# Layer 1's three modulation products: two of them out of the RWKV recurrence, one to the routing, one to the latent's mLSTM, one ahead of layer 1

## The chip, the core and the metric

The kernel runs on one core of one Trainium2 chip. The metric is the device time of one launch in microseconds (us); lower is better. One core has a matrix engine (PE in the profile; its weight loads are PEld), three engines for elementwise work (DVE, ACT, POOL), and SP, which here issues the loads of weights. Each engine runs its instructions in the order in which the program put them.

## The reference

One token sequence of 256 tokens and width 1024 goes through two blocks. Block 1 is RWKV-7 time mixing with its recurrence `wkv7_scan`, a dense SwiGLU, block attention (MoBA) and a mixture of 8 experts. Block 2 has two layers on the latent `x` and a context `xc` of 256 tokens. Every norm of block 2 is modulated by a vector that comes from a product with a large matrix:

```python
silu_c = jax.nn.silu(c)
silu_cc = jax.nn.silu(c_ctx)
for l in range(DEPTH):
    mod_x = (silu_c @ ada_w[l] + ada_b[l])[:, None, :]
    mod_c = silu_cc @ ada_w[l] + ada_b[l]
    sh1, sc1, g1, sh2, sc2, g2 = jnp.split(mod_x, 6, axis=-1)
    hx = modulate(rms_norm(x, norm_g[l, 0]), sh1, sc1)
    ...
```

`ada_w[l]` is 1024 x 6144, 25 MB in f32, and it meets two vectors only. Layer 0 of block 2 is neighbourhood attention beside a bidirectional mLSTM (`even_mixer`), layer 1 is multi-head latent attention (`odd_mixer`); each has a convolutional FFN behind it.

## The kernel before, in words

All weights come from HBM in f32, 512 KB at a time, into a ring of six buffers (`wraw`); ACT and DVE split each into a high and a low part (`whi`, `wlo`), and PE multiplies with both, so a linear layer is three sums of products (high by high, high by low, low by high). SP issues a load into a ring buffer as soon as the buffer's last reader is done; it works through its loads strictly in their order.

The modulation is cut into six products `ada(l, j)` (line 1310), j a third of layer l's columns. One has eight steps: each loads 1 MB of `ada_w` into two ring buffers, which PE reads directly, in plain f32: four matmuls of 128 rows, 32 columns and 512 elements, one to each quarter of the PSUM tile's partitions (line 1320, helper L262). After the eighth, ACT copies the PSUM tile (`adar`), PE turns it with four transposes (helper L282), and DVE adds the bias into `modT`. That is the ninth step. The PSUM tile, one of the four of set 1, is held from the first step to the last.

`Filler` (line 1334) holds the six products as generators, in the order (0,0), (0,1), (0,2), (1,0), (1,1), (1,2). `st["fill"].step(n, keep)` advances the first one by up to n steps, and stops when only `keep` products are left. The places of the calls set where the steps are written: eight in `rwkv_proj`; in `block1_front` one at every `ADA_EVERY`-th yield of the recurrence `wkv` (304 yields) up to yield 286, and one at every second from there; then at the end of `moba` and in `moe_route` (the routing).

A scheduling layer then orders what each engine gets: it keeps the written order as a priority but lets an instruction go ahead where it reckons that an engine would wait. So a step's four matmuls are often parted.

From line 2056 on, the latent's chain (`x_chain`: PSUM set 0) and the context's (`ctx_rest`: set 1) are interleaved by the numbers of `SIDE`: for each yield of the latent, so many of the context's. The context's FFN of layer 0 so runs beside the latent's mLSTM (`mlstm`, line 1601, called in `even_x`, line 1764) and beside the border between the layers (`x_chain`, lines 1995 and 1996), where the latent goes through the residual, a norm (squares on ACT: tile `sq`), a scaling on DVE (`xscr`) and transposes on PE before layer 1's first product, with `od_w_dq` (its matmuls show as `hT0h,whi`; the context's up-projections as `hT1h,whi`, down-projections as `whi,hid`).

Of the kernel before, what the change touches and what calls it, by code (L numbers as in the profile page):

```python
# [574 lines left out]
    yield  # L575


ADA_EVERY = 10
WKV_END = 286
A_RATES = (1.0, 0.8, 1.0, 0.0)  # L580
WKV_AR = 3
# [466 lines left out]
def moe_route(N, st, ch=0):  # L1048

    nc, a, c = N.nc, N.a, N.c  # L1050
    h = st["h"]
    x = N.act_slots(2, 3, "h3T")
    N.to_T(ch, lambda tb: h[:, tb * D:(tb + 1) * D], x)
    st["fill"].step(1)
    yield
    w = N.wload(a["moe_router"][0], KD, NE)
    p = N.ps(ch)
    N.mmT(p[:NE, 0:T], w, x, KD, 0, NE)
    lg = N.t256("lg")
    N.act(lg[:NE], p[:NE, 0:T])  # L1060
    p2 = N.ps(ch)
    for tb in range(2):
        N.tr(p2[:, tb * NE:(tb + 1) * NE], lg[:NE, tb * P:(tb + 1) * P])
    lt = N.cstp.tile([P, 2, NE], F32, name="logits")
    N.act(lt, p2[:, 0:2 * NE].rearrange("p (b e) -> p b e", b=2))
    st["fill"].step(2)
    yield

    gt, eq = N.t256("gt8"), N.t256("eq8")
    g4 = gt[:, 0:128].rearrange("p (b e f) -> p b e f", b=2, e=NE)  # L1070
    e4 = eq[:, 0:128].rearrange("p (b e f) -> p b e f", b=2, e=NE)
    le, lf = bc(lt, 3, NE), bc(lt, 2, NE)
    N.tt(g4, lf, le, ALU.is_gt)
    N.tt(e4, lf, le, ALU.is_equal)
    N.tt(e4, e4, bc(c["lt8"].rearrange("p (e f) -> p e f", e=NE), 1, 2), ALU.mult)
    N.tt(g4, g4, e4, ALU.add)
    rank = N.sm(16, "rank").rearrange("p (b e) -> p b e", b=2)
    nc.vector.tensor_reduce(rank, g4, axis=AX.X, op=ALU.add)
    s1 = N.sm(16, "sel1").rearrange("p (b e) -> p b e", b=2)
    s2 = N.sm(16, "sel2").rearrange("p (b e) -> p b e", b=2)  # L1080
    N.ts(s1, rank, 0.0, op0=ALU.is_equal)
    N.ts(s2, rank, 1.0, op0=ALU.is_equal)
    v = N.sm(4, "topv")
    tmp = N.sm(16, "topt").rearrange("p (b e) -> p b e", b=2)
    for i, s in ((0, s1), (1, s2)):
        N.tt(tmp, s, lt, ALU.mult)
        nc.vector.tensor_reduce(v[:, 2 * i:2 * i + 2], tmp, axis=AX.X, op=ALU.add)
    yield
    d = N.sm(2, "topd")
    N.tt(d, v[:, 2:4], v[:, 0:2], ALU.subtract)  # L1090
    N.act(d, d, AF.Exp)
    w1 = N.sm(2, "w1")
    N.ts(w1, d, 1.0, op0=ALU.add)
    nc.vector.reciprocal(w1, w1)
    w2 = N.sm(2, "w2")
    N.tt(w2, d, w1, ALU.mult)
    gates = N.cstp.tile([P, 2, NE], F32, name="gates")
    sel = N.cstp.tile([P, 2, NE], F32, name="sel")
    pos = N.cstp.tile([P, 2, NE], F32, name="pos")
    N.tt(gates, s1, bc(w1, 2, NE), ALU.mult)  # L1100
    N.tt(tmp, s2, bc(w2, 2, NE), ALU.mult)
    N.tt(gates, gates, tmp, ALU.add)
    N.tt(sel, s1, s2, ALU.add)
    p = N.ps(ch)
    st["fill"].step(100)
    N.mm(p[:, 0:NE], c["tri_strict"], sel[:, 0, :], True, True)
    N.mm(p[:, NE:2 * NE], c["ones"], sel[:, 0, :], True, False)
    N.mm(p[:, NE:2 * NE], c["tri_strict"], sel[:, 1, :], False, True)
    N.mm(p[:, 2 * NE:3 * NE], c["ones"], sel[:, 0, :], True, False)
    N.mm(p[:, 2 * NE:3 * NE], c["ones"], sel[:, 1, :], False, True)  # L1110
    nc.vector.tensor_copy(pos, p[:, 0:2 * NE].rearrange("p (b e) -> p b e", b=2))
    yield
    mx = N.sm(1, "maxn")
    nc.vector.tensor_reduce(mx, p[:, 2 * NE:3 * NE], axis=AX.X, op=ALU.max)
    cnt = N.cstp.tile([P, 1], I32, name="count")
    nc.vector.tensor_copy(cnt, mx)
    hh, hl = N.slot(4, "h_hi", F32R), N.slot(5, "h_lo", F32R)
    for i in range(0, 2 * D, 512):
        s = slice(i, i + 512)
        N.split(hh[:, s], hl[:, s], h[:, s])  # L1120
    st.update(hh=hh, hl=hl, gates=gates, sel=sel, pos=pos, cnt=cnt)
    acc = N.slot(6, "moe_acc")
    st["acc"] = acc
    yield
# [252 lines left out]
def modulated(N, st, ch, src, l, which, r, slots, scr):  # L1377

    q = 3 * which
    sc = N.sm(8, "scale")  # L1380
    N.ts(sc, st["mod"].piece(l, q + 1, r), 1.0, op0=ALU.add)
    N.tt(sc, sc, N.v["norm_g_2"][:, (l * 4 + 2 * which) * 8:(l * 4 + 2 * which) * 8 + 8], ALU.mult)
    sh = N.sm(8, "shift")
    N.nc.vector.tensor_copy(sh, st["mod"].piece(l, q, r))
    for tb in range(2):
        s = slice(tb * D, (tb + 1) * D)
        rs = inv_rms(N, src[:, s])
        N.ts(scr[:, s], src[:, s], rs)
    x = N.act_slots(slots[0], slots[1], f"hT{ch}")
    N.to_T(ch, lambda tb: scr[:, tb * D:(tb + 1) * D], x, scale=sc, bias=sh)  # L1390
    return x
# [368 lines left out]
def even_x(N, st, ch, x, S):  # L1760
    nc, a, c = N.nc, N.a, N.c
    yield from even_proj(N, st, ch, x, S, "Ex")
    E, Ec = st["Ex"], st["Ec"]
    yield from paced(mlstm(N, st, ch, E, st["CT"], st["ms"], True), SIDE["mlstm"])

    bias = [N.slot(S["b"][i], f"bias{i}") for i in range(2)]
    for jt in range(2):
        for rr in range(2):
            r0 = 7 - 2 * jt - rr
            nc.scalar.dma_start(bias[jt][rr * 64:rr * 64 + 64].rearrange("p (h x) -> p h x", h=8),  # L1770
                                a["rpb"][:, :, r0:r0 + 4].rearrange("q h r k -> q h (r k)"))
    o = N.act_slots(S["h"][0], S["h"][1], "yx")
    mlstm_out(N, st, ch, E, o)
    yield 8 * SIDE["bias"]
    qo, kv, kvc = E["qo"], E["kv"], Ec["kv"]

    def score(pr, hh, qt, p):
        q = slice(hh * 64, hh * 64 + 64)
        l = qo[q, pr * T + qt * P:pr * T + (qt + 1) * P]
        N.mm(p[:, 0:T], l, kv[q, pr * T:(pr + 1) * T], True, True)  # L1780
        N.mm(p[:, T:2 * T], l, kvc[q, pr * T:(pr + 1) * T], True, True)

    def vsrc(pr, hh, b):
        t = kv if b < 2 else kvc
        o_ = 1024 + (b % 2) * 512 + (2 * pr + hh) * 64
        return t[:, o_:o_ + 64]

    def biased(pr, hh, qt, p, S_):
        h = 2 * pr + hh
        N.stt(S_[:, 0:T], p[:, 0:T], 0.125, bias[qt][:, h * T:(h + 1) * T], ALU.mult, ALU.add)  # L1790
        N.act(S_[:, T:2 * T], p[:, T:2 * T], AF.Copy, scale=0.125)
    yield from paced(attend(N, ch, o, 4, 4, score, vsrc, 0.125, biased, ch2=1 - ch), SIDE["na"])
    st["yx_act"] = o
# [187 lines left out]
SIDE = dict(moba_in=0, moba=1, moba_out=0, start=5, mlstm=1.25, bias=0.5, na=0.5, res0=3, end0=5, mla=1.5)  # L1981


def x_chain(N, st, out, ch=0):

    a, nc = N.a, N.nc
    h = st["h"]
    x = modulated(N, st, ch, h, 0, 0, 0, (2, 3), N.slot(4, "xscr"))
    yield SIDE["start"]
    yield from even_x(N, st, ch, x, dict(qo=4, kv=5, ml=6, kh=12, h=(2, 3), b=(6, 10)))  # L1990
    yield from out_proj(N, st, ch, st["yx_act"], a["ev_w_out_2"][0], h, 0, 0, 4)
    y = N.slot(12, "ffy0")
    x = modulated(N, st, ch, h, 0, 1, 0, (2, 3), y)
    yield SIDE["res0"]
    yield from ffn_conv(N, st, ch, h, 0, 0, x, (4, 5, 6), (12, 10), y)
    x = modulated(N, st, ch, h, 1, 0, 0, (2, 3), N.slot(4, "xscr2"))
    yield SIDE["end0"]
    N.load_consts("consts_m", small(N, "consts_m"))
    yield from mla_x(N, st, ch, x, dict(lat=4, q=(5, 6), k=(12, 7), v=13, o=(2, 3)))
    yield from out_proj(N, st, ch, st["ox_act"], a["od_w_o_2"][0], h, 1, 0, 4)  # L2000
    y = N.slot(12, "ffy1")
    x = modulated(N, st, ch, h, 1, 1, 0, (2, 3), y)
    yield
    yield from ffn_conv(N, st, ch, h, 1, 0, x, (4, 5, 6), (12, 10), y,
                        lambda tb: nc.sync.dma_start(out[tb * P:(tb + 1) * P], h[:, tb * D:(tb + 1) * D]))
# [13 lines left out]
def paced(g, n):  # L2019
    for _ in g:  # L2020
        yield n
# [11 lines left out]
def block1_front(N, st):  # L2033

    ada_setup(N, st)
    fill = st["fill"] = Filler(ada(N, st, l, j) for l, j in ((0, 0), (0, 1), (0, 2), (1, 0), (1, 1), (1, 2)))
    for _ in rwkv_proj(N, st):
        pass
    for i, _ in enumerate(wkv(N, st)):
        if i % ADA_EVERY == 3 if i < WKV_END else i % 2:  # L2040
            fill.step(1, 1)
    side = ctx_even(N, st)
    for g, r in zip((rwkv_out, ffn_dense, moba, moe_route), A_RATES):
        rated(g(N, st), side, r)
    advance(side, 1000)
# [25 lines left out]
```

## Time and profile before

| | us |
|---|---|
| median of 3 runs | 2863.96 (2863.25 to 2868.87) |
| the profiled execution | 2869.28 |
| its span in the trace | 2867.5 |
| PE busy in the span | 2763.4 (96%) |
| DVE busy | 2243.2 (78%) |
| ACT busy | 1773.8 (62%) |

The span runs from the first to the last instruction of the trace; the profiled execution is 1.8 us longer, and that stays as it is. All rows below are of this execution. A row of the timeline gives the start, the time until the group's last instruction ends, engine, line, operation, what it writes and reads, its form and how many there are; in brackets the idle time of the engine before it and what ended it. An f32 matmul stands in the trace as two rows, so a step's four matmuls are x8. A busy PE is one with a matmul under way; successive matmuls overlap, so the distance from start to start is what one costs the next.

### The profile page before, as it was taken

The numbers are of one execution on the slowest core, as the hardware profiler recorded it, in microseconds if no ns is written. First come the engines' busy times: TensorE is split into PE (matmuls) and PEld (weight loads), VectorE is DVE, ScalarE is ACT, GpSimd is POOL, SyncE is SP. The second block draws the span as 40 slices with busy tenths as digits, with TensorE's granted clock in tenths as the row PEclk, the third lists the DMA queues.
The fourth block names the chain that finished last, engine by engine and source line by source line (L and its number), as shares of the span: only waits on it lengthen the run. The fifth ranks groups of instructions, "written<-read, shape, count | busy, mean of one in ns | idle before, by whom it ended". The sixth has DMA issues, their size and how long they took to land. (4 is left out here: it accounts for less than half of the span.)

```text
span 2867.5 us, 49977 instructions
## 1 busy us (share of the span) xinstructions
PE 2763.4 (96%) x18356; PEld 2268.0 (79%) x18356; DVE 2243.2 (78%) x4406; ACT 1773.8 (62%) x3601; POOL 67.0 (2%) x87
## 2 busy tenths in 40 slices
PE   8999999999999999999999999989989999989898
PEld 8677589897866777777777777768877899877897
DVE  7366385577577999999999999986687787886767
ACT  5223255444566887887787878766446665666654
POOL 0011100000000000000000000000000000000000
PEclk9999999999999999999999999999999999999999
DMA  7444666544539999999999999976543465521453
GB/s 244 161 142 155 214 193 183 178 139 134 158 96 336 357 333 352 348 356 335 346 361 335 346 349 361 348 250 176 162 129 114 137 198 178 158 78 45 147 185 125
DMA packets 357231, 641.16 MB, mean 224 GB/s; under 512 B 24785, under 2 KB 153937, under 8 KB 356978
## 3 DMA queue, kind: packets, MB, share of 16 engines
q1 hardware_dynamic: 348768, 625.58, 64.8%
q10 hardware_dynamic: 8210, 12.30, 1.4%
q8 instruction: 146, 2.39, 0.3%
q14 instruction: 107, 0.88, 0.1%
HBM read 636.76 MB, written 1.05 MB: 222 GB/s over the span
## 5 line engine op out<-in xcount | busy, mean ns | idle before, releaser
L250 DVE TENSOR_TENSOR wlo<-wraw,whi 128x512 fp32r<-128x512 f32 (+1 forms) x2181 | 1377.8, 685 | 259.0 <-ACT whi L247 198.3
L247 ACT ACTIVATE whi<-wraw 128x512 fp32r<-128x512 f32 (+1 forms) x2181 | 1215.0, 622 | 428.7 <-PE ps L262 320.9
L262 PE MATMUL ps<-whi,xg 128*128 128x512 f32 x1792 | 499.2, 398 | 1.9 <-ACT whi L247 1.9
L262 PEld LDWEIGHTS ps<-whi,xg 128*128 128x128 f32 x1792 | 327.2, 188 | 86.0 <-ACT whi L247 25.0
L262 PE MATMUL ps<-wlo,xg 128*128 128x512 f32 x896 | 295.1, 398 | 0.0
L262 PE MATMUL ps<-whi,hT 128*128 128x512 f32 x896 | 260.2, 401 | 0.0
L262 PE MATMUL ps<-hT0h,whi 128*128 128x256 f32 (+2 forms) x872 | 216.7, 286 | 3.8 <-ACT whi L247 3.3
L262 PE MATMUL ps<-hT0l,whi 128*128 128x256 f32 (+2 forms) x872 | 216.7, 285 | 0.1
L262 PEld LDWEIGHTS ps<-wlo,xg 128*128 128x128 f32 x896 | 168.1, 188 | 55.9 <-DVE wlo L250 20.4
L262 PE MATMUL ps<-whi,hid 128*128 128x512 f32 x704 | 190.4, 406 | 10.3 <-DVE cv L259 7.1
L262 PEld LDWEIGHTS ps<-whi,hT 128*128 128x128 f32 x896 | 164.4, 188 | 32.6
L262 PEld LDWEIGHTS ps<-hT0h,whi 128*128 128x128 f32 (+2 forms) x872 | 168.2, 193 | 4.9 <-ACT whi L247 3.5
L262 PEld LDWEIGHTS ps<-hT0l,whi 128*128 128x128 f32 (+2 forms) x872 | 168.3, 193 | 0.9 <-DVE hT0l L250 0.4
L262 PE MATMUL ps<-wlo,hT 128*128 128x512 f32 x448 | 168.5, 416 | 0.0
L262 PEld LDWEIGHTS ps<-whi,hid 128*128 128x128 f32 x704 | 131.7, 191 | 45.0 <-issue 15.6
L262 PE MATMUL ps<-hT1h,whi 128*128 128x256 f32 (+1 forms) x504 | 127.7, 290 | 12.2 <-ACT whi L247 11.6
L259 DVE SCALAR_TENSOR_TENSOR cv<-ps,vecs,cv 128x255 f32<-128x255 f32 x264 | 124.8, 479 | 12.7 <-ACT cv L247 11.5
L262 PE MATMUL ps<-hT1l,whi 128*128 128x256 f32 (+1 forms) x504 | 125.7, 286 | 0.0
L262 PE MATMUL ps<-hT0h,wlo 128*128 128x256 f32 (+2 forms) x872 | 123.9, 283 | 1.6 <-DVE wlo L250 1.5
L262 PEld LDWEIGHTS ps<-hT0h,wlo 128*128 128x128 f32 (+2 forms) x872 | 113.0, 191 | 2.8 <-DVE wlo L250 2.4
L262 PEld LDWEIGHTS ps<-hT1h,whi 128*128 128x128 f32 (+1 forms) x504 | 96.1, 191 | 15.0 <-ACT whi L247 13.6
L262 PEld LDWEIGHTS ps<-wlo,hT 128*128 128x128 f32 x448 | 84.2, 188 | 28.9 <-DVE wlo L250 11.1
(527 smaller groups left out, 4519.1 us busy)
## 6 DMA issues: line engine op xcount, KB each, us to landing
wraw<-moe_w_down SPq DMA_DIRECT2D x224, 512.0 KB, 5.6
wraw<-moe_w_gate SPq DMA_DIRECT2D x222, 512.0 KB, 5.3
wraw<-moe_w_up SPq DMA_DIRECT2D x222, 512.0 KB, 5.4
wraw<-ffn_w_up SPq DMA_DIRECT2D x154, 512.0 KB, 3.8
wraw<-ada_w SPq DMA_DIRECT2D x96, 512.0 KB, 4.7
wraw<-ffn_w_down SPq DMA_DIRECT2D x88, 512.0 KB, 4.1
wraw<-ev_w_in SPq DMA_DIRECT2D x56, 512.0 KB, 4.0
wraw<-rwkv_w_rkv SPq DMA_DIRECT2D x24, 512.0 KB, 5.0
```

The lines of the kernel that those rows point to most:

```text
L247: self.nc.scalar.activation(out, in_, f, **kw)
L250: (eng or self.nc.vector).tensor_tensor(out, x, y, op=op)
L259: (eng or self.nc.vector).scalar_tensor_tensor(out, x, s, y, op0=op0, op1=op1)
L262: self.nc.tensor.matmul(out, l, r, start=start, stop=stop)
```

## The change

`ADA_EVERY` goes from 10 to 26, and the calls in the recurrence keep three products back instead of one. So (1,0) and (1,1) leave the recurrence. The calls in the routing stop when two are left: (1,0) runs there, where (1,2) ran, with the same eight steps. (1,1) gets one step behind each of the first nine yields of the latent's mLSTM, and (1,2) is written whole between the end of layer 0's FFN and the norm ahead of layer 1.

```diff
-ADA_EVERY = 10
+ADA_EVERY = 26
...
     p = N.ps(ch)
-    st["fill"].step(100)
+    st["fill"].step(100, 2)
     N.mm(p[:, 0:NE], c["tri_strict"], sel[:, 0, :], True, True)
...
-    yield from paced(mlstm(N, st, ch, E, st["CT"], st["ms"], True), SIDE["mlstm"])
+    for _ in mlstm(N, st, ch, E, st["CT"], st["ms"], True):
+        st["fill"].step(1, 1)
+        yield SIDE["mlstm"]
+    st["fill"].step(100, 1)
...
     yield from ffn_conv(N, st, ch, h, 0, 0, x, (4, 5, 6), (12, 10), y)
+    st["fill"].step(100)
     x = modulated(N, st, ch, h, 1, 0, 0, (2, 3), N.slot(4, "xscr2"))
...
         if i % ADA_EVERY == 3 if i < WKV_END else i % 2:
-            fill.step(1, 1)
+            fill.step(1, 3)
```

The order on PE in the recurrence (`wkvd`, `wkvw`, `rk_ind` and `lora_hid` are the recurrence's tiles, a step is the rows `wraw,silu_c`), a piece of the difference:

```order
 L262 MATMUL ps<-wkvd_1129,wkvd_1128 64x64 x8
 L262 MATMUL ps<-lora_hid,wkvw 128x128 x2
-L262 MATMUL ps<-wraw,silu_c 32x512 x4
 L262 MATMUL ps<-wkvd_1129 64x64 x8
 L262 MATMUL ps<-rk_ind,wkvw 128x2 x2
-L262 MATMUL ps<-wraw,silu_c 32x512
 L262 MATMUL ps<-wkvd_1128,wkvd_1129 64x64 x8
```

Such uninterrupted rows of a step's matmuls are called pieces below. In the recurrence there were 54 pieces with 128 matmuls, and there are 32 with 64; all 22 that are gone stood ahead of yield 286, and the transposes of two products, four each, go too.
In the latent's mLSTM the eight steps of (1,1) stand on PE in eight pieces among the mLSTM's own products (`bM`, `vw`, `dg`, `dw`, `mlqk`) and the context's (`hid`, `hT1h`); the last two pieces, as it is now:

```order
L262 MATMUL ps<-bM,consts 128x8
L262 MATMUL ps<-wraw,silu_c 32x512 x8
L262 MATMUL ps<-whi,hid_32671 128x512 x4
...
L262 MATMUL ps<-vw,ktok_31658 128x129 x4
L262 MATMUL ps<-whi,hid_32671 128x512
L262 MATMUL ps<-wlo,hid_32671 128x512 x2
L262 MATMUL ps<-wraw,silu_c 32x512 x4
L262 MATMUL ps<-whi,hid_32671 128x512 x3
L262 MATMUL ps<-dg,consts 128x512
```

The pieces before them are one of four matmuls behind a `dg`, one of one and one of three, one of four behind the first `bM`, one of four behind a `dg`, one of four behind the second `mlqk`; the transposes stand behind them, around the last `dg` and `dw`.

On SP, the loads at the end of the latent's FFN of layer 0 (the last two `ffn_w_down` before are the context's):

```order
-L306 DMA wraw<-ffn_w_down 128x2x512 x12
+L306 DMA wraw<-ffn_w_down 128x2x512 x10
+L1318 DMA wraw<-ada_w 128x1024 x16
+L306 DMA wraw<-ffn_w_down 128x2x512 x2
 L306 DMA wraw<-ffn_w_up 128x4x256 x4
 L306 DMA wraw<-ffn_w_down 128x2x512 x2
```

The sixteen loads of the product (1,2) stand between the latent's last down-projection weights and the context's next ones. On PE at the same border, first before (`hid_36411` is the latent's hidden tile, `hid_34549` the context's, `xscr` the latent ahead of layer 1):

```order
L262 MATMUL ps<-wlo,hid_36411 128x512 x2
L262 MATMUL ps<-whi,hid_34549 128x512 x8
L262 MATMUL ps<-wlo,hid_34549 128x512 x4
L262 MATMUL ps<-whi,hid_34549 128x512 x8
L262 MATMUL ps<-wlo,hid_34549 128x512 x4
L262 MATMUL ps<-hT1h,whi 128x256
...
L282 MATMUL ps<-ident,xscr_37412 128x128 x4
```

and now (the latent's is `hid_36338`, the context's `hid_34476`):

```order
L262 MATMUL ps<-wlo,hid_36338 128x512 x2
L262 MATMUL ps<-wraw,silu_c 32x512 x32
L282 MATMUL ps<-ident,adar 128x128 x4
L262 MATMUL ps<-whi,hid_34476 128x512 x3
L282 MATMUL ps<-ident,xscr_37412 128x128 x4
L262 MATMUL ps<-whi,hid_34476 128x512 x4
L282 MATMUL ps<-ident,xscr_37412 128x128 x12
L262 MATMUL ps<-whi,hid_34476 128x512
```

All eight steps stand in one row ahead of the context's products and of the latent's transposes. On ACT the copy of this product (`adar`) now stands between the norm of the FFN's output and the squares of the norm before layer 1.

## Rows read from the trace of the kernel before

**Rows 1.** The page, part 1: busy time of each engine.
```profile
PE 2763.4 (96%) x18356; PEld 2268.0 (79%) x18356; DVE 2243.2 (78%) x4406; ACT 1773.8 (62%) x3601; POOL 67.0 (2%) x87
```

**Rows 2.** By stretch: width, PE, PEld, DVE, ACT, POOL busy, clock, DMA share, GB/s.
```profile
137.00:325.00 188.00, 186.30 (x3482) 133.03 (x3477) 107.53 (x350) 53.30 (x179) 25.24 (x36) 1.00 0.47 151
2034.00:2060.00 26.00, 26.00 (x177) 22.91 (x176) 18.27 (x45) 12.66 (x31) 0.00 (x0) 1.00 0.40 124
2060.00:2090.00 30.00, 25.67 (x163) 21.75 (x162) 28.69 (x68) 15.16 (x35) 0.00 (x0) 1.00 0.41 123
2515.00:2523.00 8.00, 6.20 (x25) 4.37 (x25) 5.22 (x12) 4.07 (x9) 1.71 (x3) 0.57 0.38 135
```

**Rows 3.** The modulation's matmuls alone, recurrence and routing (without ACT).
```profile
137.00:325.00 188.00, 45.17 (x210) 6.32 (x210) 0.00 (x0) 0.00 (x0) 1.00 0.47 151
850.00:882.00 32.00, 13.05 (x64) 2.19 (x64) 0.00 (x0) 0.00 (x0) 1.00 0.77 272
```

**Rows 4.** Timeline of PE in the recurrence: two pieces and what follows each.
```profile
154.25 1.06 PE L262 MATMUL ps<-wraw,silu_c 128*32 128x512 f32 x8
155.24 0.68 PE L262 MATMUL ps<-wkvd 64*64 64x64 f32 x16
...
156.39 1.04 PE L262 MATMUL ps<-wraw,silu_c 128*32 128x512 f32 x2
157.37 0.33 PE L262 MATMUL ps<-VS,wkvd 64*64 64x64 f32 x4
```

**Rows 5.** Timeline of DVE beside the first of these pieces.
```profile
154.80 0.41 DVE L250 TENSOR_TENSOR wkvd<-wkvd,ps 128x256 f32<-128x256 f32 x1
```

**Rows 6.** Timeline around another piece of the recurrence, PE and DVE.
```profile
247.36 1.07 PE L262 MATMUL ps<-wraw,silu_c 128*32 128x512 f32 x8
...
247.97 0.57 DVE L256 TENSOR_SCALAR wkvw<-wkvw 128x256 f32<-128x256 f32 x2 [1.05 <-ACT wkvw L247]
248.35 0.33 PE L262 MATMUL ps<-ru,wkvd 64*64 64x64 f32 x4
```

**Rows 7.** Timeline of PE in the latent's mLSTM: two waits of PE.
```profile
2080.22 1.16 PE L262 MATMUL ps<-whi,hid 128*128 128x512 f32 x4 [2.69 <-DVE dc L250]
...
2085.67 1.13 PE L262 MATMUL ps<-dg,consts 128*128 128x512 f32 x2 [0.91 <-DVE dg L250]
```

**Rows 8.** Timeline of PE at the border of the layers.
```profile
2469.45 2.03 PE L262 MATMUL ps<-whi,hid 128*128 128x512 f32 x8
...
2479.17 0.66 PE L282 MATMUL ps<-ident,xscr 128*128 128x128 f32 x4 [0.73 <-DVE xscr L254]
...
2482.29 1.53 PE L282 MATMUL ps<-ident,xscr 128*128 128x128 f32 x12 [0.31 <-DVE xscr L254]
...
2489.78 0.28 PE L262 MATMUL ps<-hT0h,whi 128*128 128x256 f32 x1
```

**Rows 9.** Timeline of SP there: the loads.
```profile
2419.47 29.00 SPq L306 DMA_DIRECT2D wraw<-ffn_w_down  x12
```

**Rows 10.** Timeline of PE: three steps in a row; a product's end.
```profile
93.83 2.78 PE L262 MATMUL ps<-wraw,silu_c 128*32 128x512 f32 x24
...
877.36 1.91 PE L262 MATMUL ps<-wraw,silu_c 128*32 128x512 f32 x12
879.97 0.66 PE L282 MATMUL ps<-ident,adar 128*128 128x128 f32 x4 [0.70 <-ACT adar L247]
```

**Rows 11.** The modulation's loads by their line, stretch 90 to 120.
```profile
DMA to landing us min/median/max: 4.3/6.7/9.2
```

**Rows 12.** As rows 2, while six such loads are under way.
```profile
98.00:104.00 6.00, 6.00 (x34) 3.63 (x36) 0.30 (x1) 0.51 (x2) 0.00 (x0) 1.00 1.02 412
```

**Rows 13.** Timeline of ACT at the border: the first square of the norm.
```profile
2474.90 0.61 ACT L247 ACTIVATE sq<-h 128x512 f32<-128x512 f32 x1
```

**Rows 14.** Timeline of PE: a wait in the routing and one behind the border.
```profile
860.94 1.05 PE L262 MATMUL ps<-wraw,silu_c 128*32 128x512 f32 x4 [2.21 <-DMA wraw<-ada_w]
...
2516.18 1.12 PE L282 MATMUL ps<-ident,cscr 128*128 128x128 f32 x4 [4.78 <-DVE cscr L254]
```

## The prediction

> **What bounds the kernel now.** The page's first part comes first: PE is busy 96% of the span, DVE 78%, ACT 62% [rows 1]. Over the whole launch PE is the bound, so a product that moves is worth what PE pays for it where it leaves, less what PE pays where it lands. Busy time by stretch tells these places apart. In the recurrence, 137 to 325, PE is busy 186.30 of 188 us and DVE 107.53, and the modulation's matmuls alone stand there with 45.17 us [rows 2, 3]. In the latent's mLSTM PE is full from 2034 to 2060 (26.00 of 26); from 2060 to 2090 DVE is the fuller engine, 28.69 of 30 against 25.67 [rows 2]. At the border of the layers the timeline shows a dense PE: from the latent's last product at 2469.45 to layer 1's first matmul at 2489.78, 20.33 us, it waits 0.73 and 0.31 us [rows 8]. So PE pays at all three places, and the question is which place adds waits to that.
>
> All sums are made against the profiled execution, 2869.28 us, which is 5.3 us above the median of the runs, 2863.96; the change is taken to be equal for both.
>
> **Part 1, the recurrence gives back 18 us.** 22 of 54 pieces go. One piece costs the next row 0.99 us (154.25 to 155.24) with four matmuls, and 0.98 (156.39 to 157.37) with one [rows 4]: the piece has the price, not the matmul. 22 x 0.98 = 21.6. Two sets of transposes go, 0.66 each [rows 10]: in all 23, the upper end. Not each piece pays in full. Beside the one at 154.25 DVE writes `wkvd`, from 154.80 to 155.21, and the next PE row reads `wkvd` at 155.24 [rows 4, 5]: without the piece PE would wait for DVE there, and nothing is won. Beside the one at 247.36 DVE writes `wkvw` only, which the next row (`ru,wkvd`) does not read [rows 6]: that piece pays in full. If half of them are of the first kind, 11 is the lower end. I take 18, nearer the upper, since PE waits for hardly anything in this stretch (1.7 us of 188) and DVE is busy for 57% of it. DVE's and SP's part of the two products (bias additions, 32 loads) goes too, and counts nothing: DVE has 80 us to spare, the DMA share is 0.47 [rows 2].
>
> **Part 2, the routing: nothing.** (1,0) has the matmuls, loads and transposes that (1,2) had, in the same place: 13.05 us of matmuls there [rows 3] stay.
>
> **Part 3, the mLSTM costs 7 us.** Eight pieces come. Five lie where PE is full, at 0.98: 4.9. One more, ahead of the DVE-bound stretch's end, pays 1.0. The last two come where PE waits for DVE, 2.69 us at 2080.22 and 0.91 us at 2085.67 [rows 7]; two steps in a row take 2 x 0.93 (three take 2.78 [rows 10]), so both fit but for some 0.2. The transposes cost 0.66 and a little. Sum 6.8, taken as 7. The cover of the last two is DVE's chain (`dc`, `dg`); gone, they cost 2.8 more. Low end 4: the DVE-bound 30 us swallow what falls into them. High end 12: the product holds one of the four PSUM tiles of set 1 and two of six ring buffers, which the context's FFN beside it uses too; no row shows what that costs, and 5 us, a piece's price once more for each of five, is my bound.
>
> **Part 4, the border costs 22 us.** (1,2) stands there as one row: eight steps ahead of everything else on PE, sixteen loads ahead of the context's weights on SP. The latent's loads are in the ring long before (the last of 12 leaves by 2448.5 [rows 9]), so six of the sixteen, three steps, are there at 2469.45 and the ring is full. The seventh leaves only when PE has read the first step's buffers, at 2469.45 + 0.93 = 2470.4. The shortest time from issue to landing of such a load is 4.3 us [rows 11]; then they follow each other at 512 KB (524288 bytes) by 412 GB/s, 1.27 us [rows 12]. The tenth of the ten lands at 2470.4 + 4.3 + 9 x 1.27 = 2486.1, and the last step ends at 2487.0. Of these 17.5 us PE works 7.4 (8 x 0.93) and waits 10.
>
> Beside that the latent's own chain stands still: ACT copies `adar` ahead of the norm's squares, which start some 0.6 us after the last step (its transposes wait 0.70 for that copy [rows 10]), 2487.6, instead of 2474.90 [rows 13]. Before, the transposes of `xscr` followed that square by 4.27 and 7.39 us (2479.17 and 2482.29 [rows 8]); now they come at 2491.9 and 2495.0, and the twelve end at 2496.3. Of the 19.3 us of PE work between 2469.45 and layer 1's first matmul (20.33 less the two waits, 1.04), only seven context products and the transposes, 3.3 us, have their place ahead of that point; the other 16.0 follow, and layer 1 begins at 2512.3 in place of 2489.8: 22.5, taken as 22. Two waits are inside this and belong to nothing else: the loads', 10 us, and that for the norm, which the context's products covered and which now stands behind the product. Low end 7: the steps' PE time and transposes alone, 8 x 0.93 + 0.66 = 8.1, less the two waits of 1.04 that they fill. High end 25.4: 22 and the clock, below. Queued behind the waiting matmuls are the context's products; behind the sixteen loads on SP the context's up and down weights, so its FFN starts again late, and DVE and ACT have no splitting to do meanwhile.
>
> The Trainium skill's page *DMA: Bandwidth & Descriptors*, section Specifications, gives a core about 358 GB/s from HBM, less than the 412 GB/s of the row; by it ten loads take an estimated 14.6 us in place of 12.7 and the border 2 us more. The measured stretch decides, and my sum goes by 412.
>
> **The sum.** -18 + 0 + 7 + 22 = **+11**: the profiled execution 2880.3, the median **2875**.
>
> **The rivals.**
> *The covers hold: faster.* One mechanism: the loads of the border's product are never late. If the ring turns over fast enough, or the step's place on PE is reached with its loads done, only PE's own time is paid there, +7; with the mLSTM's low end the sum is -18 + 4 + 7 = -7, 2857. For it speaks that three steps of eight surely find their loads; against it that six buffers hold three steps and no more, and that in the routing, where the steps also run close together, PE waits 2.21 us for `ada_w` in one place [rows 14]. It decides where the loads' waits cost less than 1.3 us, by which -7 passes the 5.7 us that count as faster (below). Chance 0.12.
>
> *The moves cancel: no change.* All 22 pieces pay (-23), and a wait behind the border, 4.78 us for the context's `cscr` [rows 14], takes up 5 of the border's 22, because the latent's late products come to lie in it: -23 + 7 + 17 = +1, 2865. For it: a PE busy for 99% of the recurrence. Against it: the context is late by the same border, so its wait moves along with it. Chance 0.25.
>
> *The clock falls in the border's waits: slower still.* Behind the wait of 4.78 us the granted clock stands at 0.57 over 2515 to 2523 [rows 2, 14], a mean between the levels of 1.2 and 2.4 GHz: at most (1 - 0.57) x 8 = 3.4 us of PE's work. The wait of 2.21 us left it at 1.00 over 850 to 882 [rows 3, 14]. Ten us of waits, in pieces of some 1 to 3 us between steps, lie between the two cases. With 3.4 the sum is +14.4, 2878. The Trainium skill's page *TensorE: Matmul & The Clock Gate*, Part 1, says that an engine that idles is gated to the lower clock and gets the full one back with activity: by it a row of matmuls that waits for each load is just the case, and it speaks against this change. Chance 0.21.
>
> That the change does not do what it says is excluded: the new order of instructions shows the pieces, loads and transposes at the four places.
>
> **How the numbers follow.** My forecast, 2875, has 0.42. The range reaches from the rival on the other side, -7, 2857, to the sum of the bad ends: recurrence -11, mLSTM +10 (its own bound of 12 with both others at their ends I hold for too much), border +25.4: +24, **2888**. Two in ten lie outside, most of them above. About 0.2%, 5.7 us, is what can be told from no change. Slower by more: forecast and clock, 0.63; within it: the cancelling case, 0.25; faster by more: 0.12.
>
> **What would show it.** In the trace of the changed kernel: the recurrence shorter by 11 to 23 us, with half the modulation's matmuls and PE still full; 2034 to 2090, placed by the latent's mLSTM, longer by about 7, with no new waits of PE for `ada_w`; at the border PE waits for `wraw<-ada_w` of about 10 us in all, spread over the last five steps, `adar` on ACT ahead of the norm's squares, and some 42 us from the latent's last product to layer 1's first matmul in place of 20.33. Wrong would be: waits under 1.3 us at the border (rival one), a recurrence that shrinks by the full 23 with a wait behind the border gone (rival two), a granted clock near 0.5 at the border (rival three), or a routing that changes.

## The result, and the profile after

The changed kernel takes 2880.78 us (median of 6 executions, 2878.17 to 2890.42), the kernel before 2866.78 beside it (6 executions, 2863.25 to 2868.87): a ratio of 1.0051, 95% interval 1.0041 to 1.0061, so slower by 14.0 us where +11 was forecast. The profiled execution is 2880.38 us with a span of 2878.6. Executions of one and the same kernel lie some 5 us to either side of their median, single ones up to 10. The profiled execution of the kernel before took 2.5 us more than this median of it, so the two traces differ by some 3 us less than the medians do.

The page's first part hardly moves, as against [rows 1]; the work is the same, and the 11.1 us by which the span has grown are almost all time in which PE is not busy:

```profile
PE 2764.0 (96%) x18356; PEld 2265.0 (79%) x18356; DVE 2241.1 (78%) x4406; ACT 1777.5 (62%) x3601; POOL 66.4 (2%) x87
```

**The recurrence.** The timeline of PE, first of the kernel before: its first and last row in this stretch, what follows the last transposes of `yz`, and the first product behind it.

```profile
137.18 0.68 PE L262 MATMUL ps<-lora_hid,wkvw 128*128 128x128 f32 x4
...
346.04 1.12 PE L282 MATMUL ps<-ident,yz 128*128 128x128 f32 x4 [4.52 <-POOL yz L250]
347.08 3.63 PE L262 MATMUL ps<-wraw,silu_c 128*32 128x512 f32 x12
351.41 1.12 PE L282 MATMUL ps<-ident,adar 128*128 128x128 f32 x4 [0.70 <-ACT adar L247]
353.15 0.79 PE L262 MATMUL ps<-whi,yTh 128*128 128x512 f32 x1 [0.62 <-ACT whi L247]
```

The same places in the changed kernel:

```profile
139.67 0.68 PE L262 MATMUL ps<-lora_hid,wkvw 128*128 128x128 f32 x4
...
323.54 0.66 PE L282 MATMUL ps<-ident,adar 128*128 128x128 f32 x4 [1.85 <-ACT adar L247]
328.74 1.12 PE L282 MATMUL ps<-ident,yz 128*128 128x128 f32 x4 [4.55 <-POOL yz L250]
329.50 0.78 PE L262 MATMUL ps<-whi,yTh 128*128 128x512 f32 x1
```

From the first row to the transposes of `yz` it is 208.86 us before and 189.07 now: 19.8 less, where 18 was forecast for the whole. Over this length PE's waits grow by 2.9 us (from 5.8 to 8.7 in sum), so a little of what the pieces gave back is waited instead. Another 6.4 us come from the end: the last six matmuls of the last product and its transposes stood behind the wait for POOL's `yz` (7.11 us from there to the first `yTh`), and the last transposes now stand ahead of it (0.76). Behind that wait they ran at a granted clock of 0.50 (345 to 354), that is at 1.2 GHz, so one and a half steps took 3.63 us, without a wait for a load. Against that the changed kernel enters the stretch 2.5 us late. In 88 to 137 its granted clock is 0.83 against 0.90 before, a mean of the two levels. This is no part of the change: up to there PE's order is the same in both kernels, and five versions below that share it enter at 136.0 to 143.1.

**The latent's mLSTM.** PE's timeline of the changed kernel, from the mLSTM's first `dw` to its last `mlqk`:

```profile
2015.58 1.10 PE L262 MATMUL ps<-dw,consts 128*128 128x512 f32 x2
...
2063.72 1.18 PE L262 MATMUL ps<-whi,hid 128*128 128x512 f32 x4 [1.39 <-DVE dc L250]
...
2098.13 1.02 PE L262 MATMUL ps<-dg,consts 128*128 128x512 f32 x2
2101.69 0.33 PE L282 MATMUL ps<-ident,adar 128*128 128x128 f32 x1 [2.53 <-ACT adar L247]
2103.83 2.08 PE L262 MATMUL ps<-dw,consts 128*128 128x512 f32 x2 [1.81 <-DVE dw L250]
2105.70 0.85 PE L282 MATMUL ps<-ident,adar 128*128 128x128 f32 x3
...
2112.34 1.06 PE L262 MATMUL ps<-mlqk 128*128 128x128 f32 x8
```

That is 96.76 us. In the kernel before the same two rows start at 2038.79 and 2120.90, 82.11 us apart:

```profile
2038.79 1.10 PE L262 MATMUL ps<-dw,consts 128*128 128x512 f32 x2
...
2113.30 1.02 PE L262 MATMUL ps<-dg,consts 128*128 128x512 f32 x2
2118.99 1.13 PE L262 MATMUL ps<-dw,consts 128*128 128x512 f32 x2
2120.90 1.05 PE L262 MATMUL ps<-mlqk 128*128 128x128 f32 x8
```

14.7 us more, against 7 forecast. From `dg` to `dw` it is 5.7 us in both; before, PE fills them with some forty of the context's products. Now the four transposes of `adar` stand behind `dg`, wait for ACT's copy, and the forty products come later: 8.5 us from `dw` to `mlqk` in place of 1.9, so 6.6 of the 14.7 us lie here.

**The border.** PE's timeline of the changed kernel; it answers to [rows 8]:

```profile
2458.87 2.78 PE L262 MATMUL ps<-wraw,silu_c 128*32 128x512 f32 x24
2463.94 1.05 PE L262 MATMUL ps<-wraw,silu_c 128*32 128x512 f32 x4 [2.29 <-DMA wraw<-ada_w]
2465.21 5.26 PE L262 MATMUL ps<-wraw,silu_c 128*32 128x512 f32 x16 [0.22 <-DMA wraw<-ada_w]
2470.70 1.05 PE L262 MATMUL ps<-wraw,silu_c 128*32 128x512 f32 x4 [0.23 <-DMA wraw<-ada_w]
2471.97 1.05 PE L262 MATMUL ps<-wraw,silu_c 128*32 128x512 f32 x4 [0.22 <-DMA wraw<-ada_w]
...
2475.82 1.05 PE L262 MATMUL ps<-wraw,silu_c 128*32 128x512 f32 x4 [0.25 <-DMA wraw<-ada_w]
2477.63 0.66 PE L282 MATMUL ps<-ident,adar 128*128 128x128 f32 x4 [0.76 <-ACT adar L247]
...
2483.00 1.53 PE L282 MATMUL ps<-ident,xscr 128*128 128x128 f32 x12 [0.68 <-DVE xscr L254]
...
2500.17 0.28 PE L262 MATMUL ps<-hT0h,whi 128*128 128x256 f32 x1
```

Three steps pass at once; from the fourth on the product goes at the pace of the loads, one half step in 1.27 us (2470.70, 2471.97), which is 512 KB at the 412 GB/s of [rows 12]. Much of this time is not idle in the trace: PE's waits for `ada_w` sum to 3.7 us, but a half step takes 1.05 us where a whole one took 0.93. ACT's timeline shows the norm behind it, its first square at 2477.47, 18.6 us behind the product's start:

```profile
2476.98 0.60 ACT L247 ACTIVATE adar<-ps 128x512 f32<-128x512 f32 x1 [16.50 <-PE ps L262]
2477.47 0.62 ACT L247 ACTIVATE sq<-h 128x512 f32<-128x512 f32 x1
```

Layer 1 begins 41.3 us (2458.87 to 2500.17) behind the latent's last product, where it was 20.33: 21.0 more. The next wait, for the context's `cscr` (4.78 us before [rows 14]), is 5.85 us now.

### The profile page after: what moved, and what is told of

Its sections match the earlier page's. It is cut to its first block, busy times and chain, and to the rows that moved or that the text cites. A ratio compares the mean times of both kernels' runs of the same rounds, so it can differ in the third digit from the quotient of the medians.

```text
span 2878.6 us, 49974 instructions
## 1 busy us (share of the span) xinstructions
PE 2764.0 (96%) x18356; PEld 2265.0 (79%) x18356; DVE 2241.1 (78%) x4406; ACT 1777.5 (62%) x3601; POOL 66.4 (2%) x87
## 3 DMA queue, kind: packets, MB, share of 16 engines
HBM read 636.76 MB, written 1.05 MB: 222 GB/s over the span
## 5 line engine op out<-in xcount | busy, mean ns | idle before, releaser
L262 PEld LDWEIGHTS ps<-whi,hid 128*128 128x128 f32 x704 | 130.8, 190 | 45.2 <-issue 14.7
L259 DVE SCALAR_TENSOR_TENSOR cv<-ps,vecs,cv 128x255 f32<-128x255 f32 x264 | 124.5, 479 | 13.7 <-ACT cv L247 12.3
```

The lines of the kernel that those rows point to most:

```text
L259: (eng or self.nc.vector).scalar_tensor_tensor(out, x, s, y, op0=op0, op1=op1)
L262: self.nc.tensor.matmul(out, l, r, start=start, stop=stop)
```

## The experiments

All times are medians of four to ten executions, each version beside the kernel before on the same chip; the brackets give the ratio to that kernel with its 95% interval.

**What each place is worth.** Two kernels leave products out: in `ada`, for the (l, j) named, only the bias is copied into `modT`.

```diff
+    if (l, j) in ((1, 2),):
+        ...
+        nc.vector.tensor_copy(dst, bc(bias, 3, 2))
+        yield
+        return
```

> Leaves out the product (1,2): its 16 loads, 32 matmuls and transposes; only the bias goes into modT. Theory (the border's product costs 21 us, and nothing of it comes back later): 2880.8 - 21 = 2860 us, and layer 1's first matmul again some 20 us after the latent's last product. Rival (a later wait, the one for the context's cscr, gives half of it back anyway): some 2870.

Measured 2857.92 us (ratio 0.9966, 0.9954 to 0.9977): 22.9 under the change. The border is as it was, 20.34 us from the first context product to layer 1:

```profile
2466.01 2.03 PE L262 MATMUL ps<-whi,hid 128*128 128x512 f32 x8
...
2486.35 0.28 PE L262 MATMUL ps<-hT0h,whi 128*128 128x256 f32 x1
```

So the border's product costs its 21 to 23 us in full, and no later wait gives any of it back: the rival with the wait for `cscr` falls. That wait is 4.79 us here and 5.85 in the change.

The same with (1,1) left out as well:

> Leaves out (1,1) and (1,2) altogether, so that of the change the recurrence alone is seen. Theory (recurrence 23 us, of which 19 lie in its body): 2866.8 - 23 = 2844, and the stretch of the latent's mLSTM as long as in the kernel before. Rival (the recurrence gives 18 as forecast, the rest is chance of the clock ahead of it): 2849.

Measured 2844.11 us (0.9912, 0.9895 to 0.9928): 22.3 under the kernel before, which is the recurrence with the routing behind it (four executions only; the interval of the ratio reaches from 21 to 30 us). Its mLSTM takes 82.44 us from `dw` to `mlqk`, as before:

```profile
2016.13 1.10 PE L262 MATMUL ps<-dw,consts 128*128 128x512 f32 x2
...
2098.57 1.05 PE L262 MATMUL ps<-mlqk 128*128 128x128 f32 x8
```

The difference of the two, 13.8 us, is the price of (1,1) in the mLSTM. The three terms are -22.3, +13.8 and +22.9. That they sum to the whole, +14.4, is no check, since each is the difference of two neighbouring versions. The traces bear the three out one by one: 26.1 us less from the recurrence's first row to `yTh`, 14.7 more in the mLSTM, 21.0 more at the border; the late start of the recurrence (2.5) and small differences of either sign make up the rest of their 11.1.

**The border's loads.** Steps four to eight read the blocks of the first three:

```diff
+            if (l, j) == (1, 2) and k >= 3:
+                raw.append(kept[2 * (k % 3) + i])
+                continue
```

> Keeps the 32 matmuls of (1,2) in their place but loads only six of its sixteen blocks; steps four to eight read the blocks of the first three steps (so these columns of the modulation are not the reference's). Theory (ten late loads hold PE up by some 10 us, the rest of the border's 21 us is PE's own time and the norm that stands behind the product): the eight steps take 7.5 us in place of 18.0, the time falls by 10 to 2871. Rival (the loads only fill a time in which the norm's chain is awaited anyhow): the time stays within 3 us of 2880.

Measured 2868.73 us (1.0005, 0.9995 to 1.0015): 12 under the change. All eight steps now pass in one row, and layer 1 begins 30.8 us behind the product's start:

```profile
2460.94 7.07 PE L262 MATMUL ps<-wraw,silu_c 128*32 128x512 f32 x64
...
2491.76 0.28 PE L262 MATMUL ps<-hT0h,whi 128*128 128x256 f32 x1
```

So of the border's 21 to 23 us, 10 (by the traces, 41.3 less 30.8) to 12 (by the medians) are late loads, and 11 are PE's time with the norm that waits behind it.

**The transposes in the mLSTM.**

```diff
-    for _ in mlstm(N, st, ch, E, st["CT"], st["ms"], True):
-        st["fill"].step(1, 1)
+    for n, _ in enumerate(mlstm(N, st, ch, E, st["CT"], st["ms"], True)):
+        if n < 8:
+            st["fill"].step(1, 1)
         yield SIDE["mlstm"]
-    st["fill"].step(100, 1)
...
     yield 8 * SIDE["bias"]
+    st["fill"].step(100, 1)
```

> The ninth step of (1,1), the copy adar, the transposes and modT, goes from inside the latent's mLSTM to behind mlstm_out. Theory (these four transposes stand on PE ahead of some forty of the context's products, wait 2.53 us for ACT's copy, and with dw behind them empty PE for over 4 us and bring the clock down): the mLSTM is 6 to 7 us shorter, 2874. Rival (the context's products are only done later, the wait is theirs to fill somewhere): under 2 us, 2879.

Measured 2877.89 us (1.0037, 1.0022 to 1.0052): 2.9 under the change, between the two, and not clear of noise, since the intervals of the two versions overlap. In the stretch itself the theory comes near: 91.37 us from `dw` to `mlqk`, 5.4 less than in the change, and the last `dw` and `mlqk` are 1.9 us apart again.

```profile
2016.77 1.10 PE L262 MATMUL ps<-dw,consts 128*128 128x512 f32 x2 [0.74 <-DVE dw L250]
...
2100.54 1.02 PE L262 MATMUL ps<-dg,consts 128*128 128x512 f32 x2
2106.23 1.12 PE L262 MATMUL ps<-dw,consts 128*128 128x512 f32 x2
2108.14 1.06 PE L262 MATMUL ps<-mlqk 128*128 128x128 f32 x8
```

Behind it, up to the end of the attention, the profiled execution loses this again, at a granted clock of 0.85 (2109 to 2202) in place of the change's 0.93 (2113 to 2206). From the last `mlqk` to the first product that reads the attention's output (`yxh`) it is 104.8 us, 97.7 in the change, and between 95.2 and 100.0 in the eight other versions that have no step of these products there. So some 5 us at least of this loss go with the moved ninth step; the rest can be chance. What stands is the split of the mLSTM's price in the stretch: 5.4 to 6.6 us for the ninth step, and 8 to 9 (91.37 less 82.44 is 8.9) for the pieces. That the ninth step costs so much over the whole run is not shown, since at its other place it cost most of this again.

**Other places for the products.** First (1,2) alone, spread over the latent's FFN:

```diff
-    yield from ffn_conv(N, st, ch, h, 0, 0, x, (4, 5, 6), (12, 10), y)
+    for n, z in enumerate(ffn_conv(N, st, ch, h, 0, 0, x, (4, 5, 6), (12, 10), y)):
+        if n % 3 == 2:
+            st["fill"].step(1)
+        yield z
```

> The change with one edit: (1,2) is written one step at every third yield of the latent's FFN of layer 0, not whole behind it. Theory (what the border pays above PE's own time is loads that come too late and a norm that stands behind them; spread, the loads are early and only 8 pieces of 1 us and the transposes are left): 2857.9 + 9 = 2867, 14 below the change. Rival (the ring and the PSUM tile are short in the FFN too, its own loads are pushed back by sixteen others): 2875 or more.

Measured 2869.91 us (1.0020, 1.0011 to 1.0030): 10.9 under the change, 12.0 above the kernel without the product, where 9 was reckoned. Nearer the theory: spread, the same product costs about half.

Then both there, a step at every second yield and at every yield behind the twentieth, and none in the mLSTM:

```diff
+        if n % 2 or n > 20:
+            st["fill"].step(1)
```

> The recurrence and the routing as in the change, (1,1) and (1,2) both in the latent's FFN of layer 0, a step at every second yield. Theory (a step costs 1 us wherever PE is full, and the mLSTM's 14 us hold 5 of waits that its transposes made): 2844 + 16 + 2 = 2862. Rival (DVE-bound mLSTM did hide some of the steps, so that the FFN is the dearer place): 2867 or more.

Measured 2863.74 us (0.9997, 0.9986 to 1.0007), nearer the theory than the rival, 17 under the change and no different from the kernel before. Two products cost the FFN 19.6 us (2863.74 less 2844.11), some 1.2 us for each of their 16 steps with all transposes; by the traces, from the FFN's first transposes of `ffy` to layer 1's first matmul, it is 21.1 us (247.0 less 225.9), 1.3 a step. All 16 lie there as whole steps, 1.00 us from start to next start:

```profile
2267.24 1.06 PE L262 MATMUL ps<-wraw,silu_c 128*32 128x512 f32 x8
2268.24 0.39 PE L262 MATMUL ps<-hT0h,whi 128*128 128x256 f32 x1
```

Last, steps set where PE waits anyway (five in the mLSTM, the rest of (1,1) behind it, (1,2) in three groups):

```diff
+    st["fill"].step(3, 1)
...
     x = modulated(N, st, ch, h, 0, 1, 0, (2, 3), y)
+    st["fill"].step(3)
...
     lat = mla_down(N, ch, x)
+    st["fill"].step(3)
```

> The recurrence and the routing as in the change; of (1,1) five steps in the latent's mLSTM, three where PE waits for the context's cv behind it, the ninth step behind mlstm_out; of (1,2) three steps where PE waits behind the transposes of the norm of the latent's FFN, two in this FFN, three where PE waits for the context's cscr in layer 1. Theory (a step costs its PE time only where PE is full; in a wait that stands anyway it is free as long as its six loads are in the ring): 2844 + 7 (seven steps at full price) + 2 (two ninth steps) = 2853. Rival (the steps delay the chain that is waited for, or their loads are late there): 2862 or more.

Measured 2866.74 us (1.0007, 0.9997 to 1.0016): the rival's side, 13.7 above the theory. PE's timeline shows what became of the three places:

```profile
2104.02 2.78 PE L262 MATMUL ps<-wraw,silu_c 128*32 128x512 f32 x24
2111.74 2.05 PE L262 MATMUL ps<-whi,hid 128*128 128x512 f32 x4 [4.94 <-DVE cv L259]
```

```profile
2236.33 2.78 PE L262 MATMUL ps<-wraw,silu_c 128*32 128x512 f32 x24
2242.75 0.63 PE L282 MATMUL ps<-ident,ffy 128*128 128x128 f32 x4 [3.64 <-DVE ss L250]
```

```profile
2505.59 0.55 PE L282 MATMUL ps<-ident,cscr 128*128 128x128 f32 x3 [1.63 <-DVE cscr L254]
```

At the first the steps stand where they were meant to, but behind them PE still waits 4.94 us, and soon after 1.04 and 1.77 more, in place of the 6.48 of the kernel without the products. At the second the scheduling layer put them ahead of the norm's transposes, not behind: 3.64 us are waited there and 2.41 a little later, in place of 0.7 and 3.3. At the third it worked: with two whole steps shortly ahead of it the wait for `cscr` is 1.63 us in place of 4.78, and the way from layer 1's first matmul to these transposes, which holds three steps, takes 26.9 us, 26.4 without the products. So at two of three places the waits of PE grew where they were to shrink; a wait is no hole of fixed size, since the steps can also move the work that it stands for.

**What a piece costs.** The products of the recurrence with half the columns, in the kernel before:

```diff
-            N.mm(p[g * 32:(g + 1) * 32, :], sc[:, k, :], raw[g // 2][:, (g % 2) * 512:(g % 2 + 1) * 512], ...)
+            w = 256 if (l, j) in ((0, 1), (0, 2), (1, 0), (1, 1)) else 512
+            N.mm(p[g * 32:(g + 1) * 32, 0:w], sc[:, k, :], raw[g // 2][:, (g % 2) * 512:(g % 2) * 512 + w], ...)
```

> The kernel before with the matmuls of the four products of the recurrence cut to half their columns (256 in place of 512 each; the columns left out are filled with others, so the output is not the reference's); loads, steps and number of matmuls stay; the order has 45 pieces in place of 54. Theory (a piece has a price of some 0.98 us that hardly hangs on what is in it): start to next start stays above 0.8 us, and the time falls by 9 to 15, mostly for the nine pieces. Rival (the price is the matmuls' columns): a piece costs 0.5 us, and the time falls by 25 or more.

Measured 2839.71 us (0.9912, 0.9895 to 0.9928), 25.7 less: the rival. One piece now costs 0.57 us with four matmuls and 0.55 with one (one row is DVE's):

```profile
156.04 0.64 PE L262 MATMUL ps<-wraw,silu_c 128*32 128x256 f32 x8
...
156.60 0.41 DVE L250 TENSOR_TENSOR wkvd<-wkvd,ps 128x256 f32<-128x256 f32 x1
156.61 0.68 PE L262 MATMUL ps<-wkvd 64*64 64x64 f32 x16
...
180.77 0.62 PE L262 MATMUL ps<-wraw,silu_c 128*32 128x256 f32 x2
181.32 0.33 PE L262 MATMUL ps<-VS,wkvd 64*64 64x64 f32 x4
```

So at these two widths a piece has the price of the columns of one of its matmuls (0.98 at 512 [rows 4], 0.56 at 256), and one to four of them side by side cost the same. Nine pieces fewer (8.8 us) and 45 pieces by 0.42 (18.9) make 27.7 us; 25.7 were measured, so nearly every piece pays. The row of `wkvd` at 156.61 is the one that stood at 155.24 before [rows 4]. It starts when DVE's write beside it starts, not when that ends: it does not read this write, and the piece ahead of it was no cover.

**Steps that are not parted.** If the number of pieces is the price, whole steps must be cheap with all products left in the recurrence. First the four matmuls as one unit for the scheduling layer, alone, in the version with both products in the FFN, and with a step at every eighth yield:

```diff
+        with N.tc.tile_critical():
             for g in range(4):
                 N.mm(p[g * 32:(g + 1) * 32, :], ...)
```

> The kernel before with one edit: the four matmuls of a step are written as one unit, which the scheduling layer may not part. The order has 32 pieces of four in the recurrence in place of 54. Theory (a piece has a price of one matmul's 512 columns, 0.98 us, however many of the four stand in it; what the change won in the recurrence was won by having 22 fewer pieces, not by moving products): 2866 - 22 = 2844, with all four products still in the recurrence. Rival (a parted step fills waits that a whole one cannot, the followers wait longer): 2856 or more.

> The same edit in the version that has (1,1) and (1,2) in the latent's FFN; 16 pieces in place of 32 in the recurrence. Theory (16 pieces of 0.98 us less): 2864 - 16 = 2848, no faster than the kernel before with whole steps, since a whole step costs the recurrence 1 us and the FFN 1.2. Rival (the recurrence is the dear place whatever the pieces): 2838 or less.

> Whole steps in the kernel before, and a step at every eighth yield of the recurrence in place of every tenth, so that its last steps do not stand behind the last transposes of yz. Theory (in the change some 6 us of the recurrence's gain came from its end: there the last steps stood behind the wait for POOL's yz, and load-bound): 2844 - 5 = 2839. Rival (the end was only the tail of the same pieces): within 2 us of whole steps alone.

Measured 2992.33, 3028.93 and 2993.04 us (ratios 1.0451, 1.0574 and 1.0454 with intervals of 0.002 to either side). These say nothing of pieces: the unit brings waits of its own. In the first of them PE waits for `ada_w` nine times between 137 and 420, 31.8 us in all, and the kernel before not once there. Such a row:

```profile
184.89 1.94 PE L262 MATMUL ps<-wraw,silu_c 128*32 128x512 f32 x8 [3.80 <-DMA wraw<-ada_w]
```

The same without a unit, by priority:

```diff
-        for g in range(4):
-            N.mm(p[g * 32:(g + 1) * 32, :], ...)
+        N.mm(p[64:96, :], sc[:, k, :], raw[1][:, 0:512], k == 0, k == KD - 1)
+        with N.tc.high_priority():
+            for g in (3, 0, 1):
+                N.mm(p[g * 32:(g + 1) * 32, :], ...)
```

> The kernel before; the first matmul of a step is now one that reads the block loaded last, and the other three follow it at a raised priority, so that they are one row without a fence that waits for others. The order has 32 pieces of four in the recurrence in place of 54, all four products still in it, and the last step stands ahead of the last transposes of yz. Theory (a piece costs 0.98 us whatever is in it; the change's gain in the recurrence is its 22 fewer pieces, and 6 us at its end): 2864 - 22 to 28 = 2836 to 2842. Rival (the products, not the pieces, are what the recurrence pays for; single matmuls filled waits of the followers): 2858 or more.

Measured 2855.85 us beside 2867.80 (0.9953, 0.9939 to 0.9966): 12 under the kernel before and some 25 under the change (28 by the ratios), faster than both with no product moved, yet only half of what the theory had. PE's waits from 136.5 to 336 show one part of the rest, `DMA wraw<-ada_w`, which is not in the list of the kernel before for its recurrence; the timeline shows another in the routing, where the longest such wait was 2.21 us before [rows 14]. The end of the recurrence stands last:

```profile
PE ps L262 <- DMA wraw<-ada_w: 3.7, 3, 2.7
```

```profile
845.91 1.93 PE L262 MATMUL ps<-wraw,silu_c 128*32 128x512 f32 x8 [3.62 <-DMA wraw<-ada_w]
```

```profile
334.96 1.12 PE L282 MATMUL ps<-ident,yz 128*128 128x128 f32 x4 [4.43 <-POOL yz L250]
335.73 0.78 PE L262 MATMUL ps<-whi,yTh 128*128 128x512 f32 x1
```

The stretch from 136.56 to the first `yTh` at 335.73 is 199.2 us there, 215.97 in the kernel before and 189.8 in the change. This version thus gets 16.8 of the 26 us that the change gains in this stretch. Not all of it is fewer pieces: the last product now ends ahead of the transposes of `yz`, as in the change, which is worth 6.3 us here too (0.77 from there to `yTh` in place of 7.11). The 22 fewer pieces are left with 10.5 us up to these transposes, where the change has 19.8, though both have 32 pieces. Of the 9.3 us between them 4.9 are longer waits of PE (13.5 in sum against 8.7), among them the 3.7 for `ada_w`. How the other 4.4 divide among two sets of transposes, the price of each piece and the clock was not tried, and no run has the grouping without the shift at the end.

## Why the prediction was right, and where it was off

- **The sign and the sum: right.** +11 forecast, +14 measured; 2880.8 us lies in the range, 2857 to 2888, and each part has the forecast's sign. That the sum came so near is in part luck: the recurrence gave 4.3 us more than forecast and the mLSTM took 6.8 more, and these errors offset each other.
- **Part 1, the recurrence: right in its mechanism, at the top of its range.** 18 forecast (11 to 23), 22.3 measured. The step that failed is the share of pieces that only cover a wait. I let a fifth of the 23 go for it; the half-column run shows that nearly all pay, and that the piece at 154.25, my example of one that does not, was misread: the tile's name does not tell which buffer the next row reads. Of the 6.4 us at the end of the stretch only one piece and one set of transposes were in a term, 1.6 us by my prices: I took the rest of the tail, its waits and its clock of 0.50, to be the same in both. And "the piece has the price, not the matmul" was half true: it doesn't matter how many matmuls a piece has, but it does how many columns one has.
- **Part 2, the routing: right.** From the first `yTh` to the last transposes in the routing it is 526.8 us before and 527.4 in the change; nothing moves by more than the executions differ.
- **Part 3, the mLSTM: the term that was mis-sized.** 7 forecast with 12 as its bound, 13.8 measured. Two steps of it failed. "The transposes cost 0.66 and a little" was 5.4 to 6.6 us in the stretch: I priced their time on PE and not what their wait for ACT does in an engine that runs in order, with forty products queued behind them that had covered DVE's chain. And the waits for `dc` and `dg`, in which two steps were to "fit but for some 0.2", hid little: the seven steps inside the stretch took 8 to 9 us, 1.1 to 1.3 each. The wait for `dc` shrank from 2.69 to 1.39 us (the row at 2063.72 of the changed kernel) and no further. The 2.8 us that the forecast sets for these two steps without their cover should be 1.7 by its own prices (2 x 0.93 less 0.2); no sum used it.
- **Part 4, the border: right, and by its own steps.** 22 forecast, 21.0 in the trace and 22.9 by the run without the product. The product's last matmul was set 17.5 us behind its start and came at 18.0 (2476.87); of that some 10 us were to be late loads, and the run with six loads gives 12 by the medians, 10 by the traces. They are not the 10 us of idle waits that the forecast wanted to see: those sum to 3.7 us, and the rest went into half steps of 1.05 us. The loads' pace is that of the row, 1.27 us; by the 358 GB/s of the Trainium skill's page *DMA: Bandwidth & Descriptors*, section Specifications, it would have been an estimated 1.46. The measurement decides.
- **The rivals.** The covers do not hold (first rival): the loads are late as reckoned. Nothing cancels later (second): its first half, that all pieces pay, came about, but without the border's product all 22.9 us are gone. The third, the clock, has the number nearest to the measured one, +14.4 (2878); its mechanism did not make it: the border took 21 to 23 us, not 25.4, and the mLSTM's excess of 6.8 us is what lifts the sum above the forecast. The clock does fall once at the border, behind the wait of 2.29 us: the granted clock is 0.91 over 2458 to 2477, a mean of the two levels (0.50, that is 1.2 GHz, from 2465.3 to 2468.7), and four half steps in a row take 5.26 us. It costs no time of its own there, since the loads set the pace of these steps anyway: the load that the next half step reads lands at 2470.65, and that half step starts at 2470.70. In the mLSTM it does: `dw`'s two matmuls take 2.08 us behind the waits, 1.13 before. The Trainium skill's page *TensorE: Matmul & The Clock Gate*, Part 1, says that an idle engine is gated to the lower clock; the trace agrees on both places, and shows that at the border, where a load sets the pace, this had no price.

## What to carry to other kernels

Here, one to four matmuls that write different quarters of a PSUM tile's partitions and follow each other directly cost what one of them costs, 0.98 to 1.00 us. So count the uninterrupted rows and not the matmuls, and try to keep them together before you move them elsewhere: the version that did so, and by it also ended its last product ahead of a long wait, was 12 us faster with nothing moved. A product that is written whole needs its loads before it starts; with a ring for three steps, the rest ran at the pace of the loads here, and everything behind it on the engine stood. When you price an instruction that is moved, ask whom it waits for at its new place, and which work behind it had been the cover of somebody else's chain.

## What the runs showed of the hardware that I had not expected

A unit that the scheduling layer must not part made the program 4.5% slower, though it held just the same four matmuls: PE waits ahead of the units, and its granted clock is 0.84 over 137 to 420, where it is 0.98 over the same time in the kernel before. Why the loads come so late for a unit was not tried.

```profile
137.00:420.00 283.00, 219.08 (x3679) 160.69 (x3678) 115.08 (x380) 58.40 (x196) 26.34 (x38) 0.84 0.33 109
```
